# Unsplit float32 operands for the routing projections and for the expert blocks beside them, in a two-layer diffusion backbone with product-key experts

## The chip, the core and the metric

The kernel runs on one core of a Trainium2 chip. The metric is device time in microseconds (us), lower is better: the time of the one launch that computes the whole reference. Every duration below is from the hardware profiler's record of one execution of the kernel before the change.

## The reference, cut to what matters

Two layers. Each has a token-mixing part (neighbourhood attention, pooling, an mLSTM) that the change leaves alone, and then an expert feed-forward part on 512 latent tokens (and, in layer 0, on 256 context tokens):

```
xn      = modulated RMSNorm(x)                          # 512 x 1024
q       = xn @ peer_wq                                  # 512 x 2048: 8 heads x 2 halves x 128
s       = q . keys           per head and half          # 512 x 128 scores, 16 such sets
top 16 of each half -> sums of candidates -> top 16     # 16 experts and gates per head: 128 per token
out     = sum over chosen experts e of  gate_e * gelu(xn . u_e) * v_e      # 16384 experts
x       = x + modulated out
```

All of it is float32, and the choice of experts hangs on small differences of scores.

## The kernel before, in words

The program is written with a framework whose scheduler sets the order of the instructions on each engine from priorities, dependences and buffer counts; each engine then runs its own queue strictly in order. TensorE is "PE", with weight loads "PEld". All DMAs below are issued from SyncE's queue ("SP").

**Float32 products.** TensorE takes two kinds of 32-bit operand here. A plain float32 product is one call, with both operands `f32`. A *split* product first cuts each operand into a rounded high part and a remainder, both of type `fp32r`, and adds three products: high x high, high x low, low x high (`mm3`, and the loop in `hidden`). For 1024 inputs, eight chunks of 128, a 512-column result takes 8 plain products or 24 split ones. The split needs its operands prepared: for a weight tile a cast on ACT (`wh`, `duh`) and a subtraction on POOL or DVE (`wl`, `dul`).

**The expert part of a layer for the latents** (`peer_lat`, L1272) runs in these steps.

1. The norm transposes the tokens and writes them, features on the partitions, as the split pair `xh`, `xl` (`norm_cols`, L360; ACT makes `xh`, POOL makes `xl`).
2. *Route* (L1060). For each of 16 *halves* (8 heads x 2): load 512 KB of `peer_wq` (`w`), split it (ACT L1085, POOL L1086), 24 products into `mm`, copy to `qt` (ACT L1106), four score products with `keysT`, copy to `S` (ACT L1111), and on DVE the top 16 of 128 for each of four token tiles (L1117 to L1126). After every four halves (two heads) comes a *pick*: for each token tile POOL adds the candidate sums (`rcd`, L1154 to L1159), DVE finds their top 16 (`rts`, `rti`, L1170 to L1178), DVE compares indices (`req`, L1182), POOL multiplies (`roh`, L1184) and DVE reduces (`ref`, L1187). Four halves and their pick are called a *turn* below; a layer has four of them.
3. *build_g*. The gates of all experts become a dense matrix by one-hot products (`go`, `gob`, PE `mm<-go,gob`), stored to HBM (`Gd`). Its first PE work is the transpose of `gif`.
4. *dense*. All 128 blocks of 128 experts are computed densely: `h` (24 split products, L1409), gelu, times the gates, and the product with `v`. Layer 0 handles 512 columns there, layer 1 handles 384; the last token tile of layer 1 and the context tokens gather their experts' rows one by one.

**Early blocks.** For 25 of the 128 blocks per layer the hidden part is computed earlier, beside route and build_g, to fill TensorE, and its gelu is stored (`Hd`, written `H` in the trace) and read back in *dense*. They are made by the generator `early` (L1415) through `hidden` (L1392), with `dul` on POOL during route and on DVE during build_g. `advance(0)` in route and `advance(8)` behind it set how many of them are handed to the scheduler where; the rest is handed out in build_g, and the scheduler mixes them by priority. In the trace their products are `sm<-...`.

What sets the order around the change is thus: the order in which the code hands out work, the buffers (`du` 2, `w` 2, `wh` and `wl` 2, `S` 2, `rwork` 2), and SP's one queue, where a load that waits for a buffer holds up all loads behind it.

Of the kernel before, what the change touches and what calls it, by code (L numbers as in the profile page):

```python
# [21 lines left out]
P = 128  # L22
# [22 lines left out]
TB = 32  # L45
UVB = 6
RH = 2
ROUTE = (0, 0)
TAIL = (8, 8)
EARLY = (tuple(range(3, 128, 5)), tuple(range(3, 128, 5)))  # L50
GSC = 32768.0
ADA_BUFS = 3
ADA_PROJ = 0.7
# [32 lines left out]
class Kern:  # L86
    def __init__(self, ctx, tc, a, dbg=None):
        self.ctx, self.tc, self.nc, self.a = ctx, tc, tc.nc, a
        self.dbg = dbg
        self.uid = 0  # L90
        self.ev = 0
        self.bg = []
        self.bg2, self.owed = None, 0.0
        self.todo = 0
        self.pace = 0.0
        self.clock = 0.0
        self.rate = 0.0
        self.gelu = False
        self.hold = False
        self.building = False  # L100

    def pool(self, st, name, bufs=1, space=None, side=None):
        kw = {}
# [255 lines left out]
    def norm_cols(self, pn, l, w, seg, xT, xs, i0):  # L359

        nc = self.nc
        for k0 in range(0, KD, 2):
            pt = self.ps("tr")
            for k in range(2):
                for q in range(2):
                    self.tr(pt[:, (2 * k + q) * P:(2 * k + q + 1) * P], xs[q][0][:, (k0 + k) * P:(k0 + k + 1) * P])
            for k in range(2):
                cs = slice(i0 * P, (i0 + 2) * P)
                two = isinstance(xT, tuple)
                o = self.T(pn, [P, 2 * P], tag="xo", bufs=3) if two else xT[:, k0 + k, cs]  # L370
                self.affine(o, pt[:, 2 * k * P:(2 * k + 2) * P],
                            self.A[l][w][:, k0 + k, seg:seg + 1], self.modT[l][:, 2 * w, k0 + k, seg:seg + 1])
                if two:
                    nc.scalar.copy(xT[0][:, k0 + k, cs], o)
                    nc.gpsimd.tensor_sub(xT[1][:, k0 + k, cs], o, xT[0][:, k0 + k, cs].bitcast(F32))
        yield
# [683 lines left out]
    def route(self, l, seg, xT, pr):  # L1060
# [5 lines left out]
        with ExitStack() as st:  # L1066
# [10 lines left out]
            picks = []  # L1077

            def weights(hp):
                raw = self.T(pq, [P, KD, P], tag="w", bufs=2)  # L1080
                self.load(raw, a["peer_wq"][l, :, hp * P:(hp + 1) * P].rearrange("(k p) n -> p k n", p=P))
                if seg:
                    return raw
                hi, lo = (self.T(pq, [P, KD, P], F32R, tag="w" + x, bufs=2) for x in "hl")
                nc.scalar.copy(hi, raw)  # L1085
                nc.gpsimd.tensor_sub(lo, raw, hi.bitcast(F32))  # L1086
                return [(hi[:, k], lo[:, k]) for k in range(KD)]

            nxt = weights(0)
            for g in range(8):  # L1090
                keys = self.T(pq, [P, 2, P], tag="keysT")
                self.load(keys, a["keysT"][l, :, 2 * g:2 * g + 2])
                for j in range(2):
                    hp = g * 2 + j
                    w, nxt = nxt, weights(hp + 1) if hp < 15 else None
                    h, s = divmod(hp, 2)
                    if seg == 0:
                        self.advance(ROUTE[l])
                    acc = self.ps("mm")
                    if seg:  # L1100
                        for k in range(KD):
                            self.mm(acc[:, :n], w[:, k], xT[:, k, :], k == 0, k == KD - 1)
                    else:
                        self.mm3(acc[:, :n], w, [(xT[0][:, k], xT[1][:, k]) for k in range(KD)])
                    qt = self.T(pq, [P, n], tag="qt")
                    nc.scalar.copy(qt, acc[:, :n])  # L1106
                    sp = self.ps("mm")
                    for i in range(nt):
                        self.mm(sp[:, i * P:(i + 1) * P], qt[:, i * P:(i + 1) * P], keys[:, j, :])
                    S = self.T(pq, [P, nt, P], tag="S", bufs=2)  # L1110
                    nc.scalar.copy(S.rearrange("p a b -> p (a b)"), sp[:, :n])  # L1111
                    wk = self.T(pq, [P, nt, P], tag="rwork", bufs=2 - seg)
                    for fn in range(5):
                        for i in range(nt):
                            v0, v1 = sf[i][:, 0, s, h, 0:8], sf[i][:, 0, s, h, 8:16]
                            if fn == 0:
                                nc.vector.max(v0, S[:, i])  # L1117
                            elif fn == 1:
                                nc.vector.match_replace(wk[:, i], in_to_replace=v0, in_values=S[:, i],
                                                        imm_value=-3.0e38)  # L1120
                            elif fn == 2:
                                nc.vector.max_index(iv[i][:, s, h, 0:8], v0, S[:, i])
                            elif fn == 3:
                                nc.vector.max(v1, wk[:, i])
                            else:
                                nc.vector.max_index(iv[i][:, s, h, 8:16], v1, wk[:, i])  # L1126
                if (g + 1) % RH == 0:
                    picks = [[self.route_pick(pq, nt, sf[i], iv[i], iota, g + 1 - RH, ts[i], ef[i])
                              for i in range(nt)]] + picks
                    for p in picks:  # L1130
                        for x in p:
                            next(x, None)
# [145 lines left out]
    def peer_lat(self, l, jobs, xt, sx, pps, after=None):  # L1278
# [3 lines left out]
        with ExitStack() as st:  # L1282
            pk = self.pool(st, "pdk", side="right")
            xh, xl = x = tuple(self.T(pk, [P, KD, SEQ], F32R, tag="x" + t) for t in "hl")
            sr, se, spu = ExitStack(), ExitStack(), ExitStack()
            run(self.norm(l, 1, 0, x, xt, side="right"))
            sx.close()
            pr = self.pool(sr, "pdr", side="left")
            self.gelu = True
            if nd < SEQ:  # L1290
                with ExitStack() as s1:
                    xT = self.T(self.pool(s1, "xT", side="right"), [P, KD, P], tag="xT")
                    ts = slice(last * P, SEQ)
                    nc.vector.tensor_add(xT, xh[:, :, ts].bitcast(F32), xl[:, :, ts].bitcast(F32))
                    xn = self.token_major(pr, xT, 0)
            pe = self.pool(se, "pe", 2)
            self.bg2 = self.early(l, pe, xh, xl)
            r = self.route(l, 0, x, pr)
            self.advance(TAIL[l])
            pv = self.pool(spu, "pv", 2, side="right")  # L1300
            self.building = True
            with ExitStack() as s1:
                self.build_g(s1, l, r)
            self.building = False
            run(self.bg2 or ())
            self.bg2 = None
            self.pu = self.pool(spu, "pu", 1, side="right")
# [88 lines left out]
    def hidden(self, l, c, pu, pool, xh, xl, tag, eng):  # L1396
# [15 lines left out]
        nc.scalar.activation(ge, hp[:, :nd], AF.Gelu_apprx_tanh)  # L1412
        return ge

    def early(self, l, pool, xh, xl):  # L1415

        for c in EARLY[l]:
            ge = self.hidden(l, c, pool, pool, xh, xl, "sm", self.nc.vector if self.building else self.nc.gpsimd)
            self.load(self.Hd[l, c], ge)
            yield  # L1420

# [282 lines left out]
```

## Time and profile before

| | |
|---|---|
| median of 3 runs | 4364.76 us (4363.22 to 4366.80) |
| the profiled execution | 4372.77 us |
| its span, first to last instruction | 4371.0 us |
| PE busy | 3977.9 us, 91% of the span |
| DVE busy | 3178.6 us, 73% |
| ACT busy | 1570.3 us, 36% |
| POOL busy | 1471.6 us, 34% |
| HBM read and written | 909.52 MB and 80.71 MB |

Busy shares are means over stages with different limits. The stages of this change, in us from the span's start: route of layer 0 from 787 to 1005, build_g 1005 to 1237, dense 1237 to 2510; for layer 1 the same from 2964 to 3185, 3388 and 4365. The columns "granted clock" (PEclk) tell how much of TensorE's full clock the throttle granted in a stretch.

### The profile page before, as it was taken

How to read it: one execution, taken by the hardware profiler on the slowest of the kernel's cores; microseconds unless marked ns; L12 is line 12 of the kernel's file. 1: busy time of each engine (PE TensorE's matmuls, PEld its weight loads, DVE VectorE, ACT ScalarE, POOL GpSimd, SP SyncE). 2: the span in 40 equal slices, each digit the busy share in tenths (PEclk: the TensorE clock that was granted, in tenths of full speed). 3: DMA queues.
4: the chain of work that ended last, by engine and by line, in shares of the span. 5: the costliest groups of instructions: out<-in, count | busy, mean ns of one | idle time of the engine just before them, and what ended most of it. 6: DMA issues, size and time to landing. Idle time of an engine off the chain costs nothing.

```text
span 4371.0 us, 57003 instructions
## 1 busy us (share of the span) xinstructions
PE 3977.9 (91%) x20829; PEld 3351.2 (77%) x20829; DVE 3178.6 (73%) x6438; ACT 1570.3 (36%) x2563; POOL 1471.6 (34%) x1264
## 2 busy tenths in 40 slices
PE   6888878878989999999999979888687999999999
PEld 4667658666878888888888868677577888888887
DVE  2444676598849999899999655665984677777775
ACT  2332243326723333233333243433274333333332
POOL 2133354680023333333333043346802122222220
PEclk8899889897999999999999989998788999999999
DMA  7663222325879999989999443123167688888884
GB/s 267 217 226 99 71 74 68 98 64 164 232 281 365 354 356 356 369 326 355 363 365 359 174 132 103 39 83 105 45 179 260 236 303 317 304 307 313 311 311 163
DMA packets 429777, 995.54 MB, mean 228 GB/s; under 512 B 31496, under 2 KB 264072, under 8 KB 376248
## 3 DMA queue, kind: packets, MB, share of 16 engines
q1 hardware_dynamic: 374200, 589.21, 39.2%
q0 software_dynamic: 55296, 402.68, 24.5%
q8 instruction: 164, 2.69, 0.2%
q14 instruction: 117, 0.96, 0.1%
HBM read 909.52 MB, written 80.71 MB: 227 GB/s over the span
## 4 chain that ended last, share of the span: by engine, by line
PE 57%; DVE 5%; issue 5%; POOL 3%; DMA 2%; ACT 1%; POOLq 0%; SPq 0%; ACTq 0%; DVEq 0%
PE o L141 26%; PE h L1409 21%; PE mm L141 7%; PE sm L1409 2%; DMA du<-in_peer_ut_dram 2%; POOL roh L1184 1%; PE tr L196 1%; POOL dul L1404 1%; POOL wl L321 0%; PE sm L141 0%; DVE req L1182 0%; DMA w<-in_w_in_dram 0%; DVE go L1383 0%; DVE go L1384 0%; DVE gob L1382 0%
## 5 line engine op out<-in xcount | busy, mean ns | idle before, releaser
L1259 POOL DMA_INDIRECT uv<-in_peer_uv_dram,ridx x384 | 628.7, 1637 | 1467.8 <-DVE eacc L1233 1309.3
L141 PE MATMUL o<-dvh,dcl 128*128 128x512 f32 x1792 | 711.0, 397 | 0.0
L141 PE MATMUL o<-dvl,dch 128*128 128x512 f32 x1792 | 707.3, 395 | 0.0
L141 PE MATMUL o<-dvh,dch 128*128 128x512 f32 x1792 | 706.2, 394 | 0.0
L1409 PE MATMUL h<-xh,duh 128*128 128x512 f32 (+1 forms) x1648 | 600.5, 364 | 16.8 <-ACT dge L1412 16.8
L1409 PE MATMUL h<-xh,dul 128*128 128x512 f32 (+1 forms) x1648 | 599.7, 364 | 0.0
L1409 PE MATMUL h<-xl,duh 128*128 128x512 f32 (+1 forms) x1648 | 599.5, 364 | 0.0
L1404 DVE TENSOR_TENSOR dul<-du,duh 128x1024 fp32r<-128x1024 f32 x228 | 278.3, 1222 | 299.2 <-ACT duh L1403 283.6
L1233 DVE SCALAR_TENSOR_TENSOR eacc<-uv,egf,eacc 128x1024 f32<-128x1024 f32 x381 | 487.5, 1280 | 0.1
L1403 ACT CAST duh<-du 128x1024 fp32r<-128x1024 f32 x256 | 268.7, 1050 | 556.6 <-PE h L1409 416.0
L1241 DVE SCALAR_TENSOR_TENSOR uv<-uv,xn 128x1024 f32<-128x1024 f32 x384 | 466.8, 1218 | 0.0
L141 PEld LDWEIGHTS o<-dvh,dcl 128*128 128x128 f32 x1792 | 336.5, 188 | 80.1 <-DVE dcl L1491 0.3
L141 PEld LDWEIGHTS o<-dvl,dch 128*128 128x128 f32 x1792 | 336.5, 188 | 78.7
L141 PEld LDWEIGHTS o<-dvh,dch 128*128 128x128 f32 x1792 | 336.4, 188 | 76.2 <-ACT dch L1490 0.2
L1477 ACT CAST dvh<-dv 128x1024 fp32r<-128x1024 f32 x256 | 263.8, 1050 | 346.4 <-PE o L141 303.6
L1478 DVE TENSOR_TENSOR dvl<-dv,dvh 128x1024 fp32r<-128x1024 f32 x256 | 309.9, 1223 | 73.3 <-ACT dvh L1477 73.2
L1409 PEld LDWEIGHTS h<-xh,duh 128*128 128x128 f32 x1648 | 311.0, 189 | 55.8 <-ACT dge L1412 18.0
L1409 PEld LDWEIGHTS h<-xl,duh 128*128 128x128 f32 x1648 | 311.1, 189 | 37.4
L1409 PEld LDWEIGHTS h<-xh,dul 128*128 128x128 f32 x1648 | 310.9, 189 | 33.0
L1490 ACT CAST dch<-dcf 128x512 fp32r<-128x512 f32 (+1 forms) x256 | 145.2, 567 | 317.0 <-DVE dcf L1487 302.2
L141 PE MATMUL mm<-go,gob 128*128 128x128 f16 x1792 | 233.3, 296 | 7.8 <-DVE go L1384 5.9
L141 PE MATMUL mm<-xh,wh 128*128 128x512 f32 (+3 forms) x560 | 223.0, 398 | 11.6 <-ACT wh L320 5.5
(359 smaller groups left out, 7690.3 us busy)
## 6 DMA issues: line engine op xcount, KB each, us to landing
du<-in_peer_ut_dram SPq DMA_DIRECT2D x256, 512.0 KB
dv<-in_peer_v_dram SPq DMA_DIRECT2D x256, 512.0 KB
Gd<-gst SPq DMA_DIRECT2D x28, 2048.0 KB
wa<-in_w_ada_dram SPq DMA_DIRECT2D x24, 2048.0 KB
w<-in_w_in_dram SPq DMA_DIRECT2D x78, 512.0 KB
dG<-Gd SPq DMA_DIRECT2D x32, 1024.0 KB
w<-in_peer_wq_dram SPq DMA_DIRECT2D x48, 512.0 KB
dG<-Gd SPq DMA_DIRECT2D x32, 768.0 KB
```

The source lines that it names most:

```text
L141: self.nc.tensor.matmul(out, lhsT=lhsT, rhs=rhs, start=start, stop=stop)
L196: self.nc.tensor.transpose(out, in_, self.ident[:n, :n])
L1184: nc.gpsimd.tensor_mul(oh, eq.rearrange("p c (h k) -> p h k c", k=16), ci[:, :, None, :].to_broadcast([P, RH, 16, NCAND]))
L1233: nc.vector.scalar_tensor_tensor(acc, t[:, D:], w, acc, op0=OP.mult, op1=OP.add)
L1241: nc.vector.scalar_tensor_tensor(t[:, :D], t[:, :D], 1.0, xn, op0=OP.mult, op1=OP.mult, accum_out=dots[:, k:k + 1])
L1259: nc.gpsimd.indirect_dma_start(t, None, a["peer_uv"], bass.IndirectOffsetOnAxis(ap=idx[:, k:k + 1], axis=0))
L1403: nc.scalar.copy(uh, u)
L1404: eng.tensor_sub(ul, u, uh.bitcast(F32))
L1409: nc.tensor.matmul(hp[:, :nd], lhsT=lt[:, k], rhs=rt[:, k, :nd], start=n == 0, stop=n == 3 * KD - 1)
L1477: nc.scalar.copy(vh, v)
L1478: nc.vector.tensor_sub(vl, v, vh.bitcast(F32))
L1490: m1 = nc.scalar.copy(ch, cf)
```

## The change

Three edits that hang together.

- **Route** takes the unsplit tokens `xf` (a new 2 MB tile that the norm fills, and from which `xh` and `xl` are made) and the raw weight tile `w`: 8 plain products a half for 24 split ones. The tiles `wh` and `wl` and their ACT and POOL instructions are gone; `w` has three buffers.
- **Early blocks beside route** come from a new generator `plain`: the first 11 (layer 0) and 13 (layer 1) early blocks, each 8 plain products of `xf` and the raw `du`. It yields after every product, and route hands out four of them (`PIECES`) in each half, between the copy to `qt` and the score products. What is left of it runs behind route.
- **The list**: 27 early blocks per layer for 25. The 16 and 14 that are left are made as before, split, with `dul` always on DVE, and are handed out in build_g.

Layer 1's gathered tile reads its tokens from `xf`, where it added `xh` and `xl` before (L1294).

```
-ROUTE = (0, 0)
-TAIL = (8, 8)
-EARLY = (tuple(range(3, 128, 5)), tuple(range(3, 128, 5)))
+EARLY = tuple(tuple(2 + (P * i) // n for i in range(n)) for n in (27, 27))
+PLAIN = (11, 13)
+PIECES = 4
...
             def weights(hp):
-                raw = self.T(pq, [P, KD, P], tag="w", bufs=2)
+                raw = self.T(pq, [P, KD, P], tag="w", bufs=3 - seg)
                 self.load(raw, a["peer_wq"][l, :, hp * P:(hp + 1) * P].rearrange("(k p) n -> p k n", p=P))
-                if seg:
-                    return raw
-                hi, lo = (self.T(pq, [P, KD, P], F32R, tag="w" + x, bufs=2) for x in "hl")
-                nc.scalar.copy(hi, raw)
-                nc.gpsimd.tensor_sub(lo, raw, hi.bitcast(F32))
-                return [(hi[:, k], lo[:, k]) for k in range(KD)]
+                return raw
...
-                    if seg == 0:
-                        self.advance(ROUTE[l])
                     acc = self.ps("mm")
-                    if seg:
-                        for k in range(KD):
-                            self.mm(acc[:, :n], w[:, k], xT[:, k, :], k == 0, k == KD - 1)
-                    else:
-                        self.mm3(acc[:, :n], w, [(xT[0][:, k], xT[1][:, k]) for k in range(KD)])
+                    for k in range(KD):
+                        self.mm(acc[:, :n], w[:, k], xT[:, k, :], k == 0, k == KD - 1)
                     qt = self.T(pq, [P, n], tag="qt")
                     nc.scalar.copy(qt, acc[:, :n])
+                    if seg == 0:
+                        self.advance(PIECES)
...
             pe = self.pool(se, "pe", 2)
+            self.bg2 = self.plain(l, pe, xf)
+            r = self.route(l, 0, xf, pr)
+            run(self.bg2 or ())
+            sf.close()
             self.bg2 = self.early(l, pe, xh, xl)
-            r = self.route(l, 0, x, pr)
-            self.advance(TAIL[l])
...
+    def plain(self, l, pool, xf):
+
+        nc = self.nc
+        nd = DENSE[l]
+        for c in EARLY[l][:PLAIN[l]]:
+            u = self.T(pool, [P, KD, P], tag="du", bufs=2)
+            self.load(u, self.a["peer_ut"][l, c])
+            hp = self.ps("sm")
+            for k in range(KD):
+                nc.tensor.matmul(hp[:, :nd], lhsT=u[:, k], rhs=xf[:, k, :nd], start=k == 0, stop=k == KD - 1)
+                if k == KD - 1:
+                    ge = self.T(pool, [P, nd], tag="dge", bufs=2)
+                    nc.scalar.activation(ge, hp[:, :nd], AF.Gelu_apprx_tanh)
+                    self.load(self.Hd[l, c], ge)
+                yield
...
-        for c in EARLY[l]:
-            ge = self.hidden(l, c, pool, pool, xh, xl, "sm", self.nc.vector if self.building else self.nc.gpsimd)
+        for c in EARLY[l][PLAIN[l]:]:
+            ge = self.hidden(l, c, pool, pool, xh, xl, "sm", self.nc.vector)
```

How it moves instructions shows on TensorE and in SP's queue at the start of layer 0's route. On TensorE, the kernel before, the end of one half's 24 products and the start of the next half's (`mm<-xh,wh` and so on are routing, `sm<-...duh` early blocks, `mm<-keysT,qt` scores):

```order
L141 MATMUL mm_6837<-xh_6638,wl_6826 128x512
L141 MATMUL mm_6837<-xh_6638,wh_6825 128x512
L141 MATMUL mm_6837<-xl_6639,wh_6825 128x512
L141 MATMUL mm_6837<-xh_6638,wl_6826 128x512
L1409 MATMUL sm_8373<-xl_6639,duh_8369 128x512
L1409 MATMUL sm_8373<-xh_6638,dul_8370 128x512
L1409 MATMUL sm_8373<-xh_6638,duh_8369 128x512
L1409 MATMUL sm_8373<-xl_6639,duh_8369 128x512
L1409 MATMUL sm_8373<-xh_6638,dul_8370 128x512
L1409 MATMUL sm_8407<-xh_6638,duh_8403 128x512
L1409 MATMUL sm_8407<-xl_6639,duh_8403 128x512
L141 MATMUL mm_6864<-keysT_6829,qt_6862 128x128 x4
```

On TensorE, the changed kernel, from the start of route on over three halves (`mm<-xf,w` routing, `sm<-xf,du` early blocks):

```order
L1417 MATMUL sm_6834<-xf_6647,du_6832 128x512 x4
L141 MATMUL mm_6821<-xf_6647,w_6815 128x512 x8
L1417 MATMUL sm_6834<-xf_6647,du_6832 128x512
L141 MATMUL mm_6839<-keysT_6817,qt_6830 128x128 x4
L141 MATMUL mm_6869<-xf_6647,w_6819 128x512 x8
L1417 MATMUL sm_6834<-xf_6647,du_6832 128x512 x3
L141 MATMUL mm_6887<-keysT_6817,qt_6878 128x128 x4
L141 MATMUL mm_6919<-xf_6647,w_6867 128x512 x8
L1417 MATMUL sm_6932<-xf_6647,du_6930 128x512 x4
L141 MATMUL mm_6937<-keysT_6915,qt_6928 128x128 x4
```

A half's routing products go from 24 to 8, and the early products between them and the scores from seven split ones to three or four plain ones.

SP's queue at the start of layer 0's route, the kernel before (`du` are early blocks' weights, `w` routing weights, `H` the store of an early block):

```order
L199 DMA iotac_6803<-in_iota_dram 128x50
L199 DMA du_8333<-in_peer_ut_dram 128x1024
L199 DMA du_8367<-in_peer_ut_dram 128x1024
L199 DMA du_8401<-in_peer_ut_dram 128x1024
L199 DMA du_8435<-in_peer_ut_dram 128x1024
L199 DMA w_6823<-in_peer_wq_dram 128x8x128
L199 DMA keysT_6829<-in_keysT_dram 128x256
L199 DMA w_6831<-in_peer_wq_dram 128x8x128
L199 DMA keysT_6953<-in_keysT_dram 128x256
```

The same place in the changed kernel:

```order
L199 DMA iotac_6795<-in_iota_dram 128x50
L199 DMA du_6832<-in_peer_ut_dram 128x1024
L199 DMA du_6930<-in_peer_ut_dram 128x1024
L199 DMA w_6815<-in_peer_wq_dram 128x8x128
L199 DMA keysT_6817<-in_keysT_dram 128x256
L199 DMA w_6819<-in_peer_wq_dram 128x8x128
L199 DMA w_6867<-in_peer_wq_dram 128x8x128
L199 DMA keysT_6915<-in_keysT_dram 128x256
L199 DMA w_6917<-in_peer_wq_dram 128x8x128
```

The first routing weights move from behind four `du` loads to behind two.

## Rows read from the trace of the kernel before

**Rows 1.** The page's chain that ended last, by engine.

```profile
PE 57%; DVE 5%; issue 5%; POOL 3%; DMA 2%; ACT 1%; POOLq 0%; SPq 0%; ACTq 0%; DVEq 0%
```

**Rows 2.** Windows by stage: us, busy PE, PEld, DVE, ACT, POOL, PEclk, DMA share, GB/s.

```profile
787.00:1005.00 218.00, 170.56 (x740) 136.40 (x740) 167.03 (x828) 63.33 (x126) 163.47 (x172) 0.88 0.26 79
1005.00:1237.00 232.00, 218.05 (x1409) 182.11 (x1408) 178.07 (x289) 159.37 (x180) 17.82 (x11) 0.92 0.77 232
1237.00:2510.00 1273.00, 1270.36 (x5496) 1034.04 (x5497) 1118.94 (x1521) 386.59 (x588) 413.74 (x254) 1.00 0.88 336
2964.00:3185.00 221.00, 160.21 (x730) 135.53 (x730) 164.28 (x833) 61.93 (x126) 162.86 (x172) 0.82 0.24 73
3185.00:3388.00 203.00, 174.93 (x1170) 160.93 (x1168) 131.19 (x213) 124.25 (x145) 30.73 (x13) 0.90 0.74 233
3388.00:4365.00 977.00, 971.82 (x4776) 866.22 (x4776) 711.38 (x942) 350.80 (x524) 208.71 (x125) 1.00 0.77 286
```

**Rows 3.** DVE's timeline: the first and last pick's start, either layer.

```profile
842.34 0.33 DVE L1170 MAX8 rts<-rcd 128x8 f32<-128x50 f32 x2 [0.98 <-POOL rcd L1156]
970.04 0.33 DVE L1170 MAX8 rts<-rcd 128x8 f32<-128x50 f32 x2 [0.84 <-POOL rcd L1156]
3021.82 0.33 DVE L1170 MAX8 rts<-rcd 128x8 f32<-128x50 f32 x2 [0.99 <-POOL rcd L1156]
3147.97 0.33 DVE L1170 MAX8 rts<-rcd 128x8 f32<-128x50 f32 x2 [0.98 <-POOL rcd L1156]
```

**Rows 4.** Plain float32 products: PE's timeline, and the context's routing by tile.

```profile
569.58 2.75 PE L141 MATMUL mm<-xT,w 128*128 128x256 f32 x12
L141 PE MATMUL mm<-xT,w x256: 377/379/764, 337.2 to 594.3; 128*128 128x256 f32 x128
```

**Rows 5.** PE's timeline: one half's four score products.

```profile
818.26 1.16 PE L141 MATMUL mm<-keysT,qt 128*128 128x128 f32 x8
```

**Rows 6.** POOL's groups in layer 0's route: busy, mean ns, idle before.

```profile
L1184 POOL TENSOR_TENSOR roh<-req,rcd 128x1600 f32<-128x1600 f16 x16 | 72.8, 4557 | 7.0 <-DVE req L1182 4.0 <-DVE ref L1187 3.0
L1086 POOL TENSOR_TENSOR wl<-w,wh 128x1024 fp32r<-128x1024 f32 x16 | 39.0, 2440 | 19.7 <-ACT wh L1085 15.7 <-DMA w<-in_peer_wq_dram 4.0
```

**Rows 7.** DVE's groups in layer 0's route.

```profile
L1182 DVE TENSOR_TENSOR req<-rtf,iota 128x1600 f16<-128x1600 f16 x16 | 31.3, 1979 | 1.2 <-POOL roh L1184 1.2
L1187 DVE TENSOR_REDUCE ref<-roh 128x32 f32<-128x1600 f32 x16 | 28.8, 1810 | 10.9 <-POOL roh L1184 10.9
```

**Rows 8.** The start of layer 0's route, timelines of SP, PE, POOL, ACT, DVE.

```profile
781.62 12.63 SPq L199 DMA_DIRECT2D du<-in_peer_ut_dram  x4
784.16 2.32 PE L196 MATMUL tr<-ident,xr 128*128 128x128 f32 x8 [0.76 <-DVE xo L136]
793.86 0.73 POOL L375 TENSOR_TENSOR xl<-xo,xh 128x256 fp32r<-128x256 f32 x1
794.62 0.38 SPq L199 DMA_DIRECT2D w<-in_peer_wq_dram  x1
799.92 1.05 ACT L1085 CAST wh<-w 128x1024 fp32r<-128x1024 f32 x1 [0.18 <-DMA w<-in_peer_wq_dram]
812.14 0.49 DVE L1117 MAX8 rsf<-S 128x8 f32<-128x128 f32 x2 [24.85 <-POOL wl L1086]
```

**Rows 9.** The first transpose of layer 0's build_g on PE.

```profile
1005.22 0.41 PE L196 MATMUL tr<-ident,gif 128*128 128x128 f32 x2
```

**Rows 10.** PE's waits in layer 1's build_g: total us, times, longest.

```profile
PE sm L1409 <- ACT duh L1403: 10.6, 5, 4.7
PE sm L1409 <- POOL dul L1404: 9.8, 2, 8.3
```

**Rows 11.** POOL's timeline in layer 1's build_g.

```profile
3318.45 10.77 POOL L1404 TENSOR_TENSOR dul<-du,duh 128x1024 fp32r<-128x1024 f32 x1 [142.64 <-ACT duh L1403]
```

**Rows 12.** DVE and POOL beside each other in layer 0's route.

```profile
892.62 4.45 POOL L1184 TENSOR_TENSOR roh<-req,rcd 128x1600 f32<-128x1600 f16 x1
894.01 3.92 DVE L1182 TENSOR_TENSOR req<-rtf,iota 128x1600 f16<-128x1600 f16 x1
```

More of the change, by code (lines that the diff above doesn't have):

```diff
@@ L99, in __init__ @@
         self.hold = False
-        self.building = False
     def pool(self, st, name, bufs=1, space=None, side=None):
@@ L369, in norm_cols @@
                 two = isinstance(xT, tuple)
-                o = self.T(pn, [P, 2 * P], tag="xo", bufs=3) if two else xT[:, k0 + k, cs]
+                if two and len(xT) < 3:
+                    o = self.T(pn, [P, 2 * P], tag="xo", bufs=3)
+                else:
+                    o = (xT[2] if two else xT)[:, k0 + k, cs]
                 self.affine(o, pt[:, 2 * k * P:(2 * k + 2) * P],
@@ L1285, in peer_lat @@
             sr, se, spu = ExitStack(), ExitStack(), ExitStack()
-            run(self.norm(l, 1, 0, x, xt, side="right"))
+            sf = ExitStack()
+            xf = self.T(self.pool(sf, "xf", 1, side="right"), [P, KD, SEQ], tag="xf")
+            run(self.norm(l, 1, 0, (xh, xl, xf), xt, side="right"))
             sx.close()
@@ L1290, in peer_lat @@
             if nd < SEQ:
[L1291 to L1295, printed above, removed]
+                xn = self.token_major(pr, xf, last)
             pe = self.pool(se, "pe", 2)
+            self.bg2 = self.plain(l, pe, xf)
+            r = self.route(l, 0, xf, pr)
+            run(self.bg2 or ())
+            sf.close()
             self.bg2 = self.early(l, pe, xh, xl)
-            r = self.route(l, 0, x, pr)
-            self.advance(TAIL[l])
             pv = self.pool(spu, "pv", 2, side="right")
-            self.building = True
             with ExitStack() as s1:
                 self.build_g(s1, l, r)
-            self.building = False
             run(self.bg2 or ())
```

## The prediction

> **What bounds the kernel now.** I read the chain of waits first: more than half of it is TensorE [rows 1], so TensorE's products are the first thing to count. A mean over the span hides where they matter, so I read windows by stage next [rows 2]. In both dense stages PE is busy all the time (1270.36 of 1273.00 us, 971.82 of 977.00): there a product taken out is time won. In route PE is busy 170.56 of 218.00 us in layer 0 and 160.21 of 221.00 in layer 1, and neither DVE (167.03) nor POOL (163.47) is full: a loop between engines sets the pace. Its beat is in DVE's timeline [rows 3]: from the first pick to the last lie three turns, (970.04 − 842.34)/3 = 42.6 us each in layer 0 and (3147.97 − 3021.82)/3 = 42.1 in layer 1. In layer 1's build_g PE is busy 174.93 of 203.00 us at a clock of 0.90, with DMA at 0.74; what it lacks there I read from its waits [rows 10].
>
> **Prices.** A split product of 512 columns costs 1270.36/5496 = 0.231 us (dense of layer 0, where PE never stops). With that, layer 1's dense, 2304 of its 4776 products being of 512 columns (those with `v`), gives (971.82 − 2304 × 0.231)/2472 = 0.178 us for one of 384 [rows 2]. The plain product is not in the trace at 512 columns, but at 256, in the context's routing: 128 products left 256 records, two each, and twelve records took 2.75 us, the last of them 0.38 long, so they follow each other at (2.75 − 0.38)/11 = 0.215 [rows 4]. Twice that for a 256-column product, twice again for 512: 0.86 us, and 0.65 for 384. The nearest other row, score products of 128 columns, gives 0.92/8 = 0.115 a record (eight records in 1.16 us, of which the last overlaps) and by width the same [rows 5]. I take 0.85 and 0.64. Bounds: below, 0.70, the three split products it stands for; above, 1.24, if a weight load of 1034.04/5497 = 0.19 us (PEld, dense of layer 0 [rows 2]) came bare before each of two records. So a plain product is dearer for TensorE than the three split ones: 0.85 against 0.69. The change can only gain elsewhere.
>
> The Trainium skill ("FP8 and Floating Point Precision", "TensorE Precision Notes") says that float32 runs as four passes, one for each pairing of the high and low parts. By that the product is 4 × 0.231 = 0.93 us; the row of 256 columns gives 0.86, so the rule holds roughly, and a half would cost about a microsecond more than I count.
>
> **Route's turns.** A half on TensorE before: 24 × 0.231 = 5.5, seven early products by the order 1.6, scores 0.9: 8.1 us, 32 a turn, well under 42.6. After, by the order: 8 routing and 4 early plain products and scores, 12 × 0.85 + 0.9 = 11.1, a turn 44.5 in layer 0; in layer 1 8 × 0.85 + 4 × 0.64 + 0.9 = 10.3, a turn 41. On DVE and POOL the turn keeps its top-16 work and the chain `req`, `roh`, `ref` (1.98, 4.56 and 1.81 us, four times a turn [rows 6, 7]); POOL loses four `wl` of 2.44 a turn, which did not fill it. So that side stays at about 42 to 44. TensorE's side and it now are nearly equal in layer 0, and two sides that hand over to each other through two `S` buffers seldom overlap fully: I take 45.5 for layer 0 and 44 for layer 1. Three turns: 3 × (45.5 − 42.6) = +9 in layer 0, 3 × (44 − 42.1) = +6 in layer 1. Bounds: −6 each, if the POOL work taken out shortens the loop; +20 in layer 0, if the product costs 0.93 and a hand-over is lost in each half.
>
> **Route's start.** Before, SP issues four `du` loads over 12.63 us, the last two waiting for POOL's `dul`, and only then the first `w` at 794.62; it is there at 799.7, 5.1 us later, is cast at 799.92, and the first top-16 starts at 812.14 [rows 8]. In the changed order two `du` loads come ahead of `w`, and neither waits for POOL; `w` waits for TensorE alone, whose last transposes end at 784.16 + 2.32 = 786.5 [rows 8]. It lands about 791.6, and 12 products and the scores bring the first `S` to about 801 and, at 11 us a half, the fourth to 833.4. The first pick follows about 6 us later, at 839.5, for 842.34: −3, though the first halves have become slower. In layer 1, with 10.3 a half, I get 3014 for 3021.82: −8. The route's total is then +6 in layer 0 (−2 to +20) and −2 in layer 1 (−8 to +8).
>
> **What remains of `plain`** behind route: 88 − 64 = 24 products in layer 0 (20 us) and 104 − 64 = 40 in layer 1 (26 us). From the last pick to build_g's first transpose lie 1005.22 − 970.04 = 35 us [rows 3, 9], in which PE has only early blocks to do: 0, and if that cover failed, at most +20.
>
> **build_g.** In layer 0 as many split products lie behind route as before (of 25 × 24 = 600, 740 − 384 − 128 = 228 lie beside route [rows 2], so 372; 16 blocks are 384): 0. In layer 1 there were 730 − 512 = 218 beside route and a few more before it, and 393 behind, now 14 × 24 = 336: 57 × 0.178 = −10, where PE sets the pace. Besides, PE waits twice for `dul` on POOL, 9.8 us, one of which is a subtraction of 10.77 us that shared its time with DVE work, and 10.6 us for `duh` [rows 10, 11]. `dul` on DVE removes the first; the second, where `du` loads are late, perhaps half. I take −18, with −30 if all of it goes and PE's clock rises from 0.90, and −10 if the waits come back behind the loads (DMA share 0.74 [rows 2]). Two blocks fewer of `gelu` and `dul` in that stage cost nothing by themselves.
>
> **dense.** Two blocks fewer have their hidden part computed: 48 × 0.231 = −11.0 in layer 0 and 48 × 0.178 = −8.5 in layer 1, since PE is the bound there [rows 2]. Two `H` tiles more are read and 512 KB `du` tiles fewer, which leaves DMA lighter. Their `duh`, `dul` go too, off the path. The dropped addition on DVE in layer 1 is a single one of 1024 columns, in the start; 0.
>
> **The sum.** Layer 0: +6 + 0 − 11 = −5. Layer 1: −2 − 18 − 8.5 = −28.5. Together −33.5. The profiled execution took 4372.77 us, of which 4371.0 are span, so 4339.3 for such a one; the runs' median lies 8.0 under it: 4331. By the terms' ends (−2 − 8 − 30 − 19.5 = −59 and +20 + 8 − 10 − 19.5 = −1.5), taken as seldom meeting, the forecast's own range is 4313 to 4350.
>
> **Rivals.**
> *No gain.* The waits of layer 1's build_g are of the loads, not of POOL: `duh` waits for `du` as before, and route's turns lengthen by the bounds' upper half. For it: DMA share 0.74 and 0.77 in build_g; against: two `dul` waits that the rows name. Sum: +15 + 6 − 5 − 19.5 = −3.5: 4361, chance 0.13. A *small gain*, between it and the forecast (4350 to 4356): 0.08.
> *Slower: the plain product's weight loads lie bare.* A product has 128 × 128 float32 weights to load for each; if that load is not hidden behind the products, two a product make it 1.24. Then a half is 15.8 us in layer 0 and 14.9 in layer 1, a turn 63 and 60, and with four turns each and the first pick late route grows by about 16 × (15.8 − 10.7) = 80 and 70, less what the first halves overlapped: about 110 in all, less 40 of dense and build_g: +70, 4435. It decides from the price at which TensorE's turn, 48 products and 3.7 of scores, passes the loop by what the rest gives, 42 us over 276 products: from about 1.03 us. Against it: at 256 columns the records follow at 0.215, so nothing lay bare. For milder forms of it, a clock that falls because route has idle time (0.88 and 0.82 there [rows 2]). Chance 0.13.
> *More gain.* DVE and POOL hold each other up: `req` takes 3.92 us beside `roh` and 1.98 on average, and one `dul` took 10.77 [rows 7, 11, 12]. With `wl` and `dul` gone from POOL (78 us over both layers by the group's 39.0 [rows 6]) the turn of DVE shrinks below 42; with TensorE at 44.5 this pays in layer 1 alone, about 3 × 4, and in both starts. 4306, chance 0.08.
> The Trainium skill ("SBUF — State Buffer", "Terms") says that VectorE and GpSimd share a port pair and that the loser blocks fully; the 10.77 us for a 2.44 us subtraction agrees, and it would speak for this rival.
>
> **How the numbers follow.** The forecast has 0.58, the rivals 0.13, 0.08, 0.13 and 0.08. What a measurement of this kernel can tell from no change is about 0.2%, 8.7 us. Faster by more than that: 0.58 + 0.08 + 0.08 = 0.74; within it 0.13; slower 0.13. The range of 8 in 10 leaves out the slower rival and the far part of the larger gain: 4306 to 4366.
>
> **What would show it.** In the profile after: a plain product of 512 columns at 0.85 us; picks 45 us apart in layer 0 and 44 in layer 1; the first `w` issued near 787; no wait of PE for `dul` on POOL in layer 1's build_g, and that stage near 185 us; dense of 1262 and 968 us. A price above 1.0, turns of 50 or more, or a build_g as long as before would prove me wrong.

## The result, and the profile after

The changed kernel takes 4406.9 us (median of 4 runs, 4399.13 to 4413.34), the kernel before 4363.99 beside it: a ratio of 1.0097, 95% interval 1.0085 to 1.0110. It is slower by some 43 us where 33 us less were forecast. The profiled execution (4399.13 us, the shortest of the four; that of before was the longest of its own) is 26.4 us of span longer, and that is divided up here.

The windows of the changed kernel by stage answer to [rows 2] (columns as there; route, build_g and dense of layer 0, then of layer 1; dense of layer 0 is cut at the last `o` here, some 11 us behind the last `h`):

```profile
782.00:1020.00 238.00, 210.54 (x575) 101.13 (x573) 166.17 (x828) 42.32 (x104) 103.67 (x148) 0.95 0.26 79
1020.00:1242.00 222.00, 213.59 (x1409) 180.52 (x1408) 180.92 (x290) 158.59 (x178) 6.19 (x6) 0.97 0.76 229
1242.00:2557.00 1315.00, 1283.94 (x5494) 1038.54 (x5494) 1121.08 (x1527) 384.56 (x586) 415.50 (x256) 0.99 0.86 328
2998.00:3239.00 241.00, 201.25 (x599) 107.23 (x597) 164.95 (x826) 41.55 (x106) 105.06 (x148) 0.92 0.25 75
3239.00:3418.00 179.00, 161.43 (x1114) 149.91 (x1115) 139.88 (x225) 120.13 (x141) 5.71 (x6) 0.90 0.76 236
3418.00:4387.00 969.00, 965.16 (x4728) 858.78 (x4728) 705.63 (x936) 347.73 (x518) 206.08 (x124) 0.99 0.78 291
```

By events of the two timelines (first instruction on the route's index table, first transpose of `gif`, first `h`, last `o`), in us:

| stage | before | after | difference | forecast |
|---|---|---|---|---|
| route, layer 0 | 231.5 | 251.2 | +19.7 | +6 |
| build_g, layer 0 | 232.0 | 221.8 | -10.2 | 0 |
| dense, layer 0 | 1283.9 | 1315.8 | +31.8 | -11 |
| route, layer 1 | 231.4 | 251.7 | +20.2 | -2 |
| build_g, layer 1 | 203.9 | 178.5 | -25.4 | -18 |
| dense, layer 1 | 971.4 | 968.7 | -2.7 | -8.5 |

The rest, -7, lies outside these stages; 5 of it ahead of layer 0's index table, which traces of kernels with the same code up to there reach at anything from 766 to 780 us. Two things cost: the routes, and dense of layer 0, in which PE now stands still for 31 us where before it stood for 3 [rows 2].

The picks, DVE's timeline of the changed kernel, answer to [rows 3]:

```profile
833.81 0.33 DVE L1165 MAX8 rts<-rcd 128x8 f32<-128x50 f32 x2 [0.99 <-POOL rcd L1151]
983.63 0.33 DVE L1165 MAX8 rts<-rcd 128x8 f32<-128x50 f32 x2 [0.98 <-POOL rcd L1151]
3047.03 0.33 DVE L1165 MAX8 rts<-rcd 128x8 f32<-128x50 f32 x2 [0.99 <-POOL rcd L1151]
3204.93 0.32 DVE L1165 MAX8 rts<-rcd 128x8 f32<-128x50 f32 x2 [0.99 <-POOL rcd L1151]
```

The turn is 149.8/3 = 49.9 us in layer 0 and 157.9/3 = 52.6 in layer 1, for 42.6 and 42.1. Over these three turns, the windows of the changed kernel:

```profile
833.80:983.60 149.80, 139.25 (x385) 66.62 (x385) 120.17 (x600) 23.77 (x66) 75.48 (x109) 0.98 0.22 67
3047.00:3204.90 157.90, 131.04 (x391) 70.12 (x390) 120.31 (x600) 24.16 (x67) 77.16 (x109) 0.91 0.21 62
```

Neither TensorE (139 of 150, 131 of 158) nor DVE (120) is full. DVE stands still for 30 and 38 us of three turns; what for shows in one turn of layer 0. First DVE, then POOL, ACT and PE:

```profile
888.28 0.98 DVE L1177 TENSOR_TENSOR req<-rtf,iota 128x1600 f16<-128x1600 f16 x1
894.25 5.13 DVE L1177 TENSOR_TENSOR req<-rtf,iota 128x1600 f16<-128x1600 f16 x1 [3.41 <-POOL roh L1179]
900.45 1.80 DVE L1182 TENSOR_REDUCE ref<-roh 128x32 f32<-128x1600 f32 x1
902.17 0.86 DVE L1112 MAX8 rsf<-S 128x8 f32<-128x128 f32 x4
889.84 8.68 POOL L1179 TENSOR_TENSOR roh<-req,rcd 128x1600 f32<-128x1600 f16 x2
890.63 0.58 ACT L1106 COPY S<-mm 128x512 f32<-128x512 f32 x1
900.62 0.22 ACT L1175 CAST rtf<-rti 128x32 f16<-128x32 uint32 x1 [9.41 <-DVE rti L1173]
900.75 0.58 ACT L1099 COPY qt<-mm 128x512 f32<-128x512 f32 x1
901.38 1.16 PE L141 MATMUL mm<-keysT,qt 128*128 128x128 f32 x8 [2.59 <-ACT qt L1099]
```

A half's scores `S` are there at 891.2, but DVE has the third `req` and the first `ref` in front of their top-16. The `req` waits 3.41 us for the first `roh`, then takes 5.13 us beside the second, where the one before, begun ahead of the first `roh`, took 0.98. The top-16 starts at 902.17. Meanwhile ACT's queue stands at the `rtf` that waits for DVE (9.41 us), the `qt` behind it is late, and PE waits for that (2.59). In the kernel before, the top-16 stands between the second and the third `req` in this turn, and its first instructions take 0.86 us both ahead of `roh` and beside it:

```profile
845.61 2.02 DVE L1182 TENSOR_TENSOR req<-rtf,iota 128x1600 f16<-128x1600 f16 x2
847.55 0.86 DVE L1117 MAX8 rsf<-S 128x8 f32<-128x128 f32 x4
859.35 0.86 DVE L1117 MAX8 rsf<-S 128x8 f32<-128x128 f32 x4
853.08 8.96 POOL L1184 TENSOR_TENSOR roh<-req,rcd 128x1600 f32<-128x1600 f16 x2
```

So the scheduler, given another mix of work, chose another order on DVE. Writing T for one half's top-16, q for `req`, f for `ref`, layer 0's first turn reads q q T f T q q f f T f T before (the others differ by a place or two), and each of the first three q q q f T q f f f T T T after (layer 1: q q q T f q f f T f T T).

In dense of layer 0, ACT's and PE's waits between 1235 and 1760 (us in total, times, longest), the changed kernel:

```profile
ACT duh L1396 <- DMA du<-in_peer_ut_dram: 72.4, 8, 13.5
PE h L1402 <- ACT dge L1405: 25.2, 8, 5.7
```

and the kernel before:

```profile
ACT duh L1403 <- DMA du<-in_peer_ut_dram: 20.1, 2, 12.0
PE h L1409 <- ACT dge L1412: 12.0, 2, 9.6
```

The wait that ended with the first `h`, ahead of the stage, is among those of PE: 9.6 of the 12.0 us before, 4.5 of the 25.2 after. The `du` loads come late. One place, timelines of ACT, SP, DVE and PE after:

```profile
1368.46 1.04 ACT L1396 CAST duh<-du 128x1024 fp32r<-128x1024 f32 x1
1382.07 2.17 SPq L199 DMA_DIRECT2D dv<-in_peer_v_dram  x2
1389.05 1.22 DVE L1397 TENSOR_TENSOR dul<-du,duh 128x1024 fp32r<-128x1024 f32 x1
1390.30 10.46 SPq L199 DMA_DIRECT2D du<-in_peer_ut_dram  x3
1398.10 1.04 ACT L1396 CAST duh<-du 128x1024 fp32r<-128x1024 f32 x1 [8.73 <-DMA du<-in_peer_ut_dram]
1399.69 0.50 PE L1402 MATMUL h<-xh,duh 128*128 128x512 f32 x1 [2.69 <-ACT dge L1405]
```

Three `du` stand in one bunch behind the `dv` loads, are issued only from 1390.30, and the first of them has its cast at 1398.10. The last thing that this first one waited for is not a `dv` load but its own buffer: the block that held it was cast to `duh` by 1369.5, but its `dul`, which frees the buffer, ran on DVE only from 1389.05 to 1390.27. DVE was busy for 19.98 of the 20 us from 1370 on, with other work in front of that `dul`.

### The profile page after: what moved, and what is told of

Same layout as the page of the kernel before. It is cut to its first block, busy times and chain, and to the rows that moved or that the text cites. A ratio compares the mean times of both kernels' runs of the same rounds, so it can differ in the third digit from the quotient of the medians.

```text
span 4397.4 us, 55860 instructions
## 1 busy us (share of the span) xinstructions
PE 4030.5 (92%) x20381; PEld 3256.0 (74%) x20381; DVE 3184.7 (72%) x6441; ACT 1517.1 (34%) x2507; POOL 1316.4 (30%) x1204
## 4 chain that ended last, share of the span: by engine, by line
PE 67%; DVE 15%; POOL 5%; DMA 5%; issue 5%; ACT 3%; SPq 0%; POOLq 0%; ACTq 0%; DVEq 0%
PE o L141 24%; PE h L1402 20%; PE mm L141 17%; DMA du<-in_peer_ut_dram 3%; PE sm L1402 2%; POOL roh L1179 2%; PE tr L196 1%; DVE req L1177 1%; PE sm L141 1%; PE sm L1417 1%; DMA w<-in_w_in_dram 1%; DVE eacc L1228 1%; DVE uv L1236 1%; POOL rcd L1149 1%; POOL wl L321 1%
## 5 line engine op out<-in xcount | busy, mean ns | idle before, releaser
L1396 ACT CAST duh<-du 128x1024 fp32r<-128x1024 f32 x232 | 243.6, 1050 | 596.7 <-PE h L1402 432.0
L141 PE MATMUL mm<-xf,w 128*128 128x512 f32 x512 | 231.2, 606 | 0.1
```

Source lines behind the costliest of these rows:

```text
L141: self.nc.tensor.matmul(out, lhsT=lhsT, rhs=rhs, start=start, stop=stop)
L1396: nc.scalar.copy(uh, u)
```

## Experiments

A first theory for each loss and its rival came from these rows; where a theory fell, the next is named. Times are medians; every ratio is to runs of the kernel before on the same chip.

**1. The list of early blocks.** In the changed kernel the list of before (25 blocks); in the kernel before the list of the change (27):

```
-EARLY = tuple(tuple(2 + (P * i) // n for i in range(n)) for n in (27, 27))
+EARLY = (tuple(range(3, 128, 5)), tuple(range(3, 128, 5)))      # a_list25; the reverse: b_list27
```

> The changed kernel with the 25 early blocks 3, 8, 13, ... of before for the 27 of the change; nothing else differs (11 and 13 plain ones, so 14 and 12 split ones remain). Theory A, the list sets the order in which the loads stand in SP's queue in layer 0's dense, and there three du loads are queued behind three dv loads that wait for buffers: dense of layer 0, first h to last o, goes from 1316 us back to about 1284, PE's waits there vanish, and the whole to about 4372. Rival A, dense suffers from something that the routing edit left behind (the gathers' phase, DMA near its limit): dense stays near 1316, the whole near 4405 or, by two more blocks computed, above.

> The kernel before with the 27 early blocks of the change and nothing else. Theory A (the list orders the loads badly): dense of layer 0 takes about 1310 us for 1284, the whole 4385 to 4395. Rival A (the list is harmless): two blocks fewer in each dense, -11 and -8.5, against a longer build_g, the whole 4350 to 4365.

Measured: a_list25 4358.72 us, ratio 0.9987 (0.9975 to 0.9999), dense of layer 0 1292.3 us. b_list27 4402.49, ratio 1.0086 (1.0068 to 1.0103), dense 1311.9. The list alone, with the old routing, costs nearly all of what the change costs; taken out, it gives 48 us back. What the routes cost and what build_g gains (40 and 36 us in the table) nearly cancel.

**2. Count or place.** 27 blocks with the first 13 in the places of before, and 25 with the first ten where the change has them:

```
+EARLY = (tuple(range(3, 64, 5)) + tuple(67 + (60 * i) // 14 for i in range(14)),) * 2        # a_list27late
+EARLY = (tuple(2 + (P * i) // 27 for i in range(10))
+         + tuple(50 + (78 * i) // 15 for i in range(15)),) * 2                               # a_list25front
```

> The changed kernel with 27 early blocks, the first 13 in the places of before (3, 8, ..., 63), the other 14 in steps of four and five behind. If the places of the first ten cost the time (SP's order there), dense of layer 0, first h to last o, is 1275 to 1290 us for 1316 and the whole 4360 to 4375; if the count does (DMA cannot keep up with 27), it stays at 1300 or more and the whole at 4390 or more.

> The changed kernel with 25 early blocks of which the first ten are those of the change (2, 6, 11, 16, 20, ...) and the other 15 stand five and six apart. If the places of the first ten cost the time, dense of layer 0 is at 1310 us or more and the whole at 4385 or more; if the count does, dense is near 1290 and the whole near 4359, as with the evenly spaced 25.

Measured: a_list27late 4359.29, ratio 0.9987 (0.9978 to 0.9997), dense 1275.9, that is -8.0 to before, near the forecast's -11. a_list25front 4406.24, ratio 1.0091 (1.0074 to 1.0108), dense 1340.0. Place, not count. In a_list27late as many products as after are in dense, from nearly the same start (1241 us); by 1760 us PE has run 2227 records there and 2053 after, 174 x 0.231 = 40 us more. The waits for `du` follow, in a_list27late and then in a_list25front:

```profile
ACT duh L1396 <- DMA du<-in_peer_ut_dram: 16.6, 3, 7.5
```

```profile
ACT duh L1396 <- DMA du<-in_peer_ut_dram: 67.5, 8, 14.7
```

**3. Is it the order of the loads?** In dense, the lines that load and split `v` were moved behind `hidden`, which loads `du` (list of 27 kept).

> The changed kernel with its own 27 early blocks; in dense a block's du load is put ahead of its dv load in the program, which takes the three places out of SP's queue in which three dv loads stand ahead of three du loads. Theory A, those places are what dense of layer 0 stalls on: first h to last o falls from 1316 to 1275 to 1290 us, the whole from 4407 to 4365 to 4380. Rival A2 (27 early blocks put more bytes into the same time than DMA can move, wherever the loads stand): dense stays at 1305 to 1316.

Measured: 4389.70, ratio 1.0056 (1.0039 to 1.0073); the profiled execution was the longest of its runs, with dense at 1308.5 and 75.1 us of waits for `du`. Some 17 us of the median came back, of which this trace shows 7 in dense. In it three `dv` with three `du` right behind them stand nowhere in SP's queue up to 1760 us (three times after, twice before), and the waits for `du` are as long as ever. So theory A's places are at most a part of what the stage stalls on; where the shorter runs of this kernel gained the other 10 us is not shown. Dense lies in rival A2's range, but a_list27late rules A2 out: 27 blocks at 1275.9 us. How those places delay the loads stays open; that DVE frees the `du` buffers late, as in the rows above, is a candidate that no run tests.

**4. Routing alone.** The kernel before with `xf` and raw `w` in route and nothing else of the change:

```
-                        self.mm3(acc[:, :n], w, [(xT[0][:, k], xT[1][:, k]) for k in range(KD)])
+                        self.mm(acc[:, :n], w[:, k], xT[:, k, :], k == 0, k == KD - 1)
```

> The kernel before with the routing projections alone unsplit (xf and raw w, no wh and wl); the early blocks are those of before, split, handed out as before, dul on POOL during route. Theory B: TensorE has about 9.5 us of work a half with the split early products, 38 a turn, ahead of DVE; turns of 42 to 44, the first top-16 some 5 us earlier, the whole 4345 to 4365. Rival B (the plain product itself makes route long): turns of 48 or more and a whole above 4385.

Measured: 4391.69, ratio 1.0068 (1.0047 to 1.0090), turns of 47.6 and 47.3 us, though TensorE is busy for only 38 of them. The whole is near rival B's, but with 9 us to spare in each turn the plain product's price can't be the reason, and theory B's turns of 42 to 44 didn't come either. The scheduler chose yet another order on DVE here (layer 0: q f T q q f T q f f T T, then twice q q T q f q T f f f T T).

**5. ACT's casts.** `rtf` on DVE for ACT:

> The changed kernel with one cast of each pick (rtf) on DVE for ACT. Theory B, ACT's queue holds rtf, which waits for DVE, ahead of the copy qt, for which TensorE waits: the waits of PE for qt in route (9 us in each turn of layer 1, 2.6 in layer 0) go, turns fall from 50 and 52.5 us to about 46 and 44, the whole by some 35 us to about 4370. Rival B, the turn is TensorE's own work (16 records of 0.43 us for routing, 8 for the early block, 0.9 for scores, 45 us) and its lower clock: turns stay within 1 us of 50 and 52, the whole at 4400 to 4410.

Measured: 4419.18, ratio 1.0127 (1.0106 to 1.0148), turns of 51.5 and 51.3. Theory B fell: with `rtf` gone from ACT, the cast `rsf`, which waits for DVE just as well, holds `qt` back (PE waited 8.0 us for it in one turn), and the small cast itself took 7.78 us on DVE beside POOL's `roh`. POOL, then DVE, ACT and PE in that turn of layer 1:

```profile
3130.81 8.71 POOL L1179 TENSOR_TENSOR roh<-req,rcd 128x1600 f32<-128x1600 f16 x2
3131.78 7.78 DVE L1175 CAST rtf<-rti 128x32 f16<-128x32 uint32 x1
3148.29 0.17 DVE L1175 CAST rtf<-rti 128x32 f16<-128x32 uint32 x1
3165.79 1.01 ACT L1143 ACTIVATE rsf<-riv 128x32 f32<-128x32 uint32 x4 [15.06 <-DVE riv L1121]
3167.55 2.08 PE L141 MATMUL mm<-keysT,qt 128*128 128x128 f32 x8 [8.04 <-ACT qt L1099]
```

Both point at DVE's order, which still has three `req` ahead of the first top-16 here.

**6. DVE's order.** The order within a turn was forced: each `req`, `ref` and first top-16 instruction is issued after the one named before it (`issue_after`), half by half. a25_order_b puts the order of before on the changed kernel (with the 25 blocks), b_order_a that of the change (one place off layer 0's, where the first `ref` stands ahead of the top-16, and one off layer 1's) on the kernel before, b_order_b its own order on the kernel before.

```
+TURN = ((0, 1), (0,), (2, 3, 1, 2), (3,), ())      # order_b: tiles advanced ahead of half 0 and behind halves 0 to 3
+TURN = ((0, 1, 2), (0, 3, 1, 2, 3), (), (), ())    # order_a
...
+                for i in TURN[m + 1]:
+                    with self.tc.issue_after(last.ins):
+                        last = next(picks[0][i])
```

> The changed kernel with the 25 early blocks of before, and DVE's order within a turn of the latents' route forced to that of before: two compares (req), top-16 of a half, a reduction (ref), top-16, two compares, two reductions, top-16, reduction, top-16; the scheduler had put three compares first and three top-16 last. Theory C, that order makes DVE wait for POOL's roh with nothing to do: turns fall from 50 and 52.5 us to 45 to 46 in layer 0 and 43 to 45 in layer 1, the whole from 4359 to 4320 to 4335. Rival B, TensorE's work and clock make the turn: it stays above 49, the whole 4350 to 4365.

> The kernel before, split as it was, with DVE's order within a turn forced to that which the scheduler chose for the changed kernel (three compares, top-16, reduction, compare, three reductions, three top-16). Theory C: turns of 42.6 and 42.1 us become 48 to 51, the whole 4395 to 4420. Rival B (the order is harmless, the plain product makes the turn): turns of 42 to 44, the whole within 10 us of before.

> The kernel before with its own DVE order of most turns forced in the same way as the other orders were. If forcing has no effect of its own, turns stay at 42 to 43 and the whole within 10 us of before; if it has, that must be taken off the other two runs with a forced order.

Measured: a25_order_b 4328.93, ratio 0.9925 (0.9908 to 0.9941); b_order_a 4446.18, ratio 1.0190 (1.0173 to 1.0207); b_order_b 4373.02, ratio 1.0018 (1.0008 to 1.0027), with turns of 44.2 and 44.0 us: forcing gains nothing by itself and costs some 8 us. First and last pick of a25_order_b in layer 0 and layer 1:

```profile
838.69 0.32 DVE L1185 MAX8 rts<-rcd 128x8 f32<-128x50 f32 x2 [0.99 <-POOL rcd L1171]
977.33 0.32 DVE L1185 MAX8 rts<-rcd 128x8 f32<-128x50 f32 x2 [0.99 <-POOL rcd L1171]
3002.07 0.33 DVE L1185 MAX8 rts<-rcd 128x8 f32<-128x50 f32 x2 [0.98 <-POOL rcd L1171]
3139.88 0.32 DVE L1185 MAX8 rts<-rcd 128x8 f32<-128x50 f32 x2 [0.98 <-POOL rcd L1171]
```

and of b_order_a in layer 0:

```profile
839.74 0.33 DVE L1190 MAX8 rts<-rcd 128x8 f32<-128x50 f32 x2 [0.99 <-POOL rcd L1176]
1004.80 0.33 DVE L1190 MAX8 rts<-rcd 128x8 f32<-128x50 f32 x2 [0.99 <-POOL rcd L1176]
```

Turns of 46.2 and 45.9 with the old order on the new kernel, 55.0 with the new order on the old one. Over a25_order_b's three turns PE is busy 97% in layer 0:

```profile
838.70:977.30 138.60, 135.09 (x385) 65.17 (x384) 116.02 (x600) 24.12 (x66) 75.72 (x109) 1.00 0.24 73
```

That is what the forecast had taken for granted: TensorE the bound, at 45 and a little.

**7. The same wait from ACT's side, and TensorE's share.** All three index casts on POOL (a25_poolcast, and with the forced order a25_best, and alone on the kernel before, b_poolcast); and `PIECES = 0` (a25_pieces0).

```
-        nc.scalar.activation(sf[:, 1, 0, hs], iv[:, 0, hs], AF.Copy, scale=128.0)
+        nc.gpsimd.tensor_scalar(sf[:, 1, 0, hs], iv[:, 0, hs], 128.0, None, op0=OP.mult)
...
-        nc.scalar.copy(tf, ti.rearrange("p h k -> p (h k)"))
+        nc.gpsimd.tensor_copy(tf, ti.rearrange("p h k -> p (h k)"))
```

> The changed kernel with the 25 early blocks of before and with all three index casts of a pick (twice rsf, rtf) on POOL for ACT, so that ACT's queue holds only copies for TensorE and gelus. Theory B2, ACT's casts that wait for DVE keep qt back and so make the turn: turns of 45 to 46 in layer 0, 43 to 45 in layer 1, the whole about 4325. Theory C, DVE's order makes it: turns of 48 to 51, since the order here still has most top-16 behind the pick; the whole 4345 to 4365.

> The changed kernel with the 25 early blocks of before, where route hands out no early products (all of the plain ones run behind route): TensorE has 8 products and the scores a half, 31 us a turn for 45. Rival B: the turn falls by 7 us and more, to 43 or less. Theory C: it stays at 46 to 50, set by DVE and POOL. The whole is longer, since 88 and 104 products lie bare behind route.

> The changed kernel with the 25 early blocks of before, DVE's order forced to that of before and the index casts on POOL for ACT. Either alone gave 46.2 and 45.9 (order), 47.5 and 44.9 (casts) a turn. TensorE's own work is 44.8 and 41 us: if both waits are gone and TensorE is the bound, 45 in layer 0 and 42 to 43 in layer 1, the whole 4310 to 4322; if what is left is DVE and POOL's own work, no better than the better of the two, 4322 to 4330.

> The kernel before with the index casts on POOL for ACT and nothing else. If ACT's casts cost time only where TensorE has little slack (it has 32 us of work in a turn of 42.6 here), turns stay at 42 to 43.5 and the whole within 8 us of before. If they lengthen any turn, turns of 39 to 40 and a whole some 15 to 20 us shorter.

Measured: a25_poolcast 4326.76, ratio 0.9923 (0.9907 to 0.9940), turns of 47.5 and 44.9: as good as the order, and near theory B2's numbers. But its DVE order changed too (q q f T q q f f f T T T in layer 0), with two `req` ahead of the first top-16 again, so the run doesn't tell the casts from the order. a25_pieces0: 4377.18 in one run, turns of 46.3 and 45.8, and another DVE order again: TensorE runs 312 and 342 records in three turns for 385 and 391, is busy for 37 and 39 us of a turn, and the turn is still 46. Both together, a25_best, gave 4332.16, ratio 0.9926 (0.9909 to 0.9942), turns of 47.0: no more than either. The three turns of layer 0 and layer 1 in a25_poolcast, then in a25_best, columns as in [rows 2]:

```profile
831.40:974.00 142.60, 142.60 (x404) 69.06 (x404) 108.17 (x601) 18.86 (x32) 79.98 (x145) 1.00 0.25 76
3002.90:3137.70 134.80, 134.80 (x423) 72.67 (x422) 107.86 (x601) 19.63 (x34) 80.03 (x145) 1.00 0.28 84
840.00:980.90 140.90, 140.90 (x400) 68.31 (x399) 107.97 (x600) 18.22 (x31) 78.17 (x145) 1.00 0.26 77
3007.90:3148.90 141.00, 141.00 (x443) 76.31 (x442) 108.03 (x601) 19.73 (x34) 78.31 (x145) 1.00 0.29 88
```

PE doesn't stand still in any of them: TensorE's work is the bound. Its records are more than after (400 and 443 for 385 and 391) because more early products fell into these turns; in layer 0 of a25_best, three turns of 44.8 us (four halves of 24 records of 0.43 and scores of 0.9) and 16 records more make 141.3 us, for 140.9. b_poolcast 4386.28, ratio 1.0056 (1.0039 to 1.0073), turns of 46.7 and 45.1: neither case came; POOL has `wl` to make there, and PE waited 25.7 us for it in layer 0's route.

**8. `dul`.** The split early blocks of build_g make `dul` on POOL again:

```
-            ge = self.hidden(l, c, pool, pool, xh, xl, "sm", self.nc.vector)
+            ge = self.hidden(l, c, pool, pool, xh, xl, "sm", self.nc.gpsimd)
```

> The changed kernel with the 25 early blocks of before, where the split early blocks that are left (in build_g) make dul on POOL for DVE. If the waits for dul on POOL were what layer 1's build_g lost in the kernel before, gif to first h grows from 158 us by 8 to 20, and layer 0's from 206 by as much; if the smaller count of products alone made it shorter, both stay within 3 us.

> The changed kernel with the 25 early blocks of before, DVE's order in a turn forced to that of before, and dul of the split early blocks on POOL. The two edits gained 30 and 15 us alone and act in different stages (route; build_g and the first blocks of dense): 4310 to 4318 if they add up, 4325 to 4330 if the second gain was of another kind.

Measured: a25_dulpool 4343.83, ratio 0.9960 (0.9945 to 0.9974); gif to first `h` 205.0 and 157.3 us, for 205.6 and 158.3 in a_list25. PE waits 1.3 us for it in layer 1. The engine was not what build_g lost in the kernel before. Its median is 15 us under that of a_list25 (13 if each is set against its own runs of the kernel before), of which the traces show 7 in dense's first blocks of layer 0 and 3 in layer 1. With the forced order, a25_opt: 4312.44, ratio 0.9877 (0.9861 to 0.9894), the shortest of all, 51 to 53 us under the kernel before: the two gains add up, as expected.

## Why the prediction was wrong, by its steps

- **The price of a plain product** was right: 16 records of the routing took 7.03 us, (7.03 - 0.59)/15 = 0.43 each, 0.86 a product (0.85 taken). The slower rival's bare weight loads did not come; the kernel became slower without them.

```profile
927.05 7.03 PE L141 MATMUL mm<-xf,w 128*128 128x512 f32 x16
```

- **Route's start** was right: the first `w` was issued behind two `du`, and the first top-16 began 26.6 us after the index table instead of 38.4.

```profile
776.79 0.81 SPq L199 DMA_DIRECT2D du<-in_peer_ut_dram  x2
781.57 0.38 SPq L199 DMA_DIRECT2D w<-in_peer_wq_dram  x1
```

Counted from there the first pick came 3.5 us earlier in layer 0 (3 forecast) and 9.3 in layer 1 (8).
- **Route's turns** are the first step that failed, in the words "So that side stays at about 42 to 44". The step took DVE's and POOL's work for a sum of durations that the change leaves alone. The durations nearly did stay (DVE is busy for 117 us of layer 0's three turns before, 120 after); their order changed, and with it the waits between them: 49.9 and 52.6 us, (49.9 - 45.5) x 3 = +13 and (52.6 - 44) x 3 = +26 over the forecast. Layer 1's route, at +20, lies outside the step's own bounds of -8 to +8. Experiment 6 shows the cause from both sides: 46.2 and 45.9 us with the old order on the new kernel, 55.0 with the new order on the old one, where its own order, forced alike, gives 44.2. That ACT's queue passes DVE's waits on to PE is in the rows; what that costs beside DVE's order, 5 and 7 don't show. (Layer 0's lower bound, -2, doesn't follow from -6 for the turns and -3 for the start; it had no part in the miss.)
- **What remains of `plain`** was right: 36.2 and 34.4 us from last pick to first transpose, as before.
- **build_g** gained more than forecast, and half of the forecast's reason was wrong. Layer 1: PE's busy time fell by 174.9 - 161.4 = 13.5 us, its idle time by 10.5. The idle part was put down to `dul` on POOL; experiment 8 brings POOL back without bringing the time back. A split block in this stage costs more than its products: from 14 to 12 of them (after against a_list25) layer 1's build_g fell from 178.5 to 158.3, 10 us a block, where its 24 products are 4.3; why was not followed up. By count alone the stage lost as much as dense won: a_list27late against a_list25 has +15.8 and +19.8 us in build_g and -16.4 and -16.9 in dense, and the two have the same ratio, 0.9987. The two blocks more, which the forecast counted as a gain of dense, were worth nothing in these places.
- **dense** of layer 0 is the second step that failed: "PE is the bound there". It was, for the old places. The step counted two blocks fewer and did not ask what other places do: with those of the change the `du` loads come late and PE stands still for 31 us (experiment 2). With 27 blocks in other places the term is there (a_list27late, -8.0).
In layer 1 the two blocks gave 2.7 of 8.5; in a_list27late's places they gave 8.9, so there too the places cost something, some 6 us.
- **The sum.** With both orders mended (and 25 blocks) the kernel takes about what was forecast (4331; a25_order_b took 4328.93), but that is luck, since the terms are others. Against before, its trace has +10.6 and 0 us in the routes (+6 and -2 forecast), -26.4 and -45.3 in build_g (0 and -18), and +7.6 and +9.9 in dense (-11 and -8.5), where it has as many blocks as before.

The larger-gain rival's port, DVE beside POOL, was seen, against the change: a `req` of 5.13 us beside `roh`, for 0.98 when begun ahead of it. The Trainium skill ("SBUF — State Buffer", "Terms") has the loser of that port pair block; the trace agrees for `req`. The top-16 instructions ran beside `roh` at their usual length, which is why their place in the order matters.

## What to carry to other kernels

Where a scheduler sets each engine's order, a change of the work on one engine can reorder another, whose own instructions it leaves alone: compare the orders of the engines that wait for each other, and look for an instruction that waits standing ahead of one that could run. A list of places is such an order too: move it alone, before it is moved with other things. A loop over four in-order queues can be slow with none of them full; its turn is read from an event that recurs, and its cause from the longest wait within one turn.

## What the runs showed of the hardware

A plain float32 product of 512 columns costs 0.86 us (the changed kernel's route), three split ones 3 x 0.231 = 0.69 (dense of the kernel before): the split is the cheaper on TensorE by a fifth, and what the plain one saves is preparation on ACT and POOL. A cast of 128 x 32 elements took 7.78 us on DVE while POOL ran two `roh`, for 0.17 when POOL was idle (a_rtf_dve).
